# Down projections of two gated feed-forward layers by Strassen's seven block products, on one core

## The chip, the cores and the metric

One Trainium2 chip, one of its cores. The metric is the device time of one execution in microseconds (us). The kernel before takes 1410.69 us as the median of three runs (1410.56 to 1411.05).

## The reference

Two decoder layers on 512 tokens with 1024 features, in float32. The mixers (a state-space scan with stick-breaking attention, then an mLSTM) are not touched by the change. Behind each mixer stands the same feed-forward block, and its down projection is what changes:

```python
def conv_ffn(h, up_w, conv_w, conv_b, down_w):
    u = causal_dwconv(h @ up_w, conv_w, conv_b)
    gate, val = jnp.split(u, 2, axis=-1)
    return (jax.nn.silu(gate) * val) @ down_w
...
        h = h + conv_ffn(rmsnorm(h, norm_w[layer, 1]), ffn_up_w[layer], ffn_conv_w[layer],
                         ffn_conv_b[layer], ffn_down_w[layer])
```

`up_w` is 1024 x 5632, `down_w` is 2816 x 1024, the convolution has width 3.

## The kernel before, in words

Activations lie with features on the 128 partitions and the 512 tokens along the free dimension: `h` is 8 tiles of 128x512, and the gated product of a feed-forward block is 22 tiles (`FF`). A tile of the program is named by what it holds, and the profile and the listings use these names.

**Three products for one.** Float32 operands are split into a rounded part and a rest, both in the type fp32r: `hi` and `lo` for weights, `sh` and `sl` for a gated tile, `xnh` and `xnl` for a normed one. `split` (L505) is a copy on ScalarE (ACT) and a subtraction on VectorE (DVE). `mm3` (L499) multiplies hi x hi, hi x lo and lo x hi into one PSUM bank, so each 128x128 block of weights costs three matmuls of 512 columns on TensorE (PE), each with its own weight load.

**Weights.** They come as units of up to 128x1024 in the order of use. `prefetch` (L482) loads a unit into one of 2 `raw` buffers (`RAW_BUFS`), ACT copies it to `hi`, DVE subtracts to get `lo`; 5 pairs of `hi` and `lo` are kept (`W_BUFS`). `unit` (L493) hands out the next pair.

**The feed-forward block** is `ffn` (L1121). For each of 22 j it forms two up tiles (gate and value): `feat` (L522) runs 24 matmuls over the 8 normed input tiles; DVE multiplies the bank with the norm's row factor `rb` (into `u`); ACT writes the first convolution tap into `c`, DVE adds the other two taps; ACT applies SiLU to the gate; DVE multiplies gate and value; `split` makes `sh`, `sl`. When all 22 are there, each of 8 output tiles takes 66 matmuls in one bank, from three weight units (`DOWN`, L97), and one DVE addition into `h[c]`. In the last block `h[c]` is then stored.

**What follows block 0** is the norm of layer 1 (`norm`, L586): for each `h[k]`, ACT and DVE make `xnh` and `xnl`, ACT squares, DVE sums into `acc`; `rstd` (L567) multiplies `acc` with a column of ones on PE (8 matmuls of 2 columns into `tt`), DVE scales (`var`), GpSimd (POOL) takes the power, DVE spreads the result (`rep`), PE transposes it 4 times. Meanwhile PE runs the first matmuls of layer 1 (`ml_v`, L974: blocks of 24 matmuls of 264 columns into banks `pj`), whose banks are emptied with the factor `rstd`.

**Banks and order.** PSUM has 8 banks: 4 for the name `pj`, 4 shared by `yy`, `zz` and `tt` (L466). The program is first recorded, then `Recorder.order` (L305) gives the instructions of all engines one order from a table of costs (`cost`, L279): at each step the engine that can start first takes its earliest ready call. That order is then fixed: every engine works its own list from front to back. The instructions are issued from one line, L422, so the profile tells them apart by tiles alone.

```python
W_BUFS = 5
RAW_BUFS = 2
SLOTS = 71
```

Of the kernel before, what the change touches and what calls it, by code (L numbers as in the profile page):

```python
# [22 lines left out]
P = 128  # L23
T = 512
# [3 lines left out]
FF = 22  # L28
# [15 lines left out]
def _units(i):  # L44

    hy, ml = i["hy_in_w"][0], i["ml_in_w"][0]
    u = []
    qw, kw, vw = hy[:, 2576:3600], hy[:, 3600:4624], hy[:, 4624:5648]
    xbc, z = _feat(hy[:, 1024:2560]), _feat(hy[:, 0:1024])
    wo = i["hy_out_w"][0]  # L50
    oa, ob = _feat(wo[:1024]), _feat(wo[1024:])
    for kind, n in [x for _, xs in L0_PLAN for x in xs]:
        if kind == "xbc":
            u.append(xbc[n])
        elif kind == "kqv":
            c = slice(P * n, P * n + P)
            dt = hy[:, 2560:2576] if n == 0 else hy[:, 0:0]
            m = np.concatenate([kw[:, c], qw[:, c], vw[:, c], dt], axis=1)
            u += _tok(m) if n else list(m.reshape(KD, P, -1))
        elif kind == "z":  # L60
            u.append(z[n])
        elif kind == "a":
            u.append(oa[n])
    u += ob
    u += _ffn_units(i, 0)
    q, k, v, o = _feat(ml[:, 0:512]), _feat(ml[:, 512:1024]), ml[:, 1024:2048], _feat(ml[:, 2048:3072])
    for kind, n in L1_ORDER:
# [12 lines left out]
    u += _feat(i["ml_out_w"][0])  # L80
    u += _ffn_units(i, 1)
    return u


def _ffn_units(i, l):
    u = []
    up = _feat(i["ffn_up_w"][l])
    for j in range(FF):
        u += [up[j], up[FF + j]]
    dn = i["ffn_down_w"][l]  # L90
    parts = [_feat(dn[a:b]) for a, b in DOWN]
    for c in range(8):
        u += [p[c] for p in parts]
    return u


DOWN = [(0, 1024), (1024, 2048), (2048, 2816)]  # L97

X = lambda kind, *ns: [(kind, n) for n in ns]
# [133 lines left out]
class Pool:  # L235
# [27 lines left out]
class Recorder:  # L263
# [165 lines left out]
W_BUFS = 5  # L429
RAW_BUFS = 2  # L430
# [4 lines left out]
class Net:  # L435
    def __init__(self, tc, pools, xT, w, sizes, pp, off, cc, out):
        self.nc = Recorder()
        self.const, self.wp, self.slots, self.small, self.psp, self.dram = pools
        self.xT, self.out = View(xT, xT.shape), View(out, out.shape)
        self.off = off  # L440
        self.w, self.sizes = View(w, w.shape), sizes
        self.wpos, self.wi = 0, 0
        self.wq = []
        self.n = 0
        nc = self.nc
        c = self.const.tile([P, C_N], F32, name="cc")
# [24 lines left out]
        o = self.off[name] + n  # L471
        return self.pp[:, o : o + w]

    def load_unit(self, tile):
        n = self.sizes[self.wi]
        src = self.w[self.wpos : self.wpos + P * n].rearrange("(p n) -> p n", p=P)
        self.wpos += P * n
        self.wi += 1
        self.nc.sync.dma_start(tile[:, 0:n], src)
        return tile[:, 0:n]  # L480

    def prefetch(self, held=0):  # L482
        nc = self.nc
        while self.wi < len(self.sizes) and len(self.wq) + held < W_BUFS:
            raw = self.load_unit(self.wp.tile([P, 1024], F32, tag="raw", bufs=RAW_BUFS, name=self.name("raw")))
            n = raw.shape[-1]
            hi = self.wp.tile([P, 1024], F32R, tag="hi", bufs=W_BUFS, name=self.name("hi"))[:, 0:n]
            lo = self.wp.tile([P, 1024], F32R, tag="lo", bufs=W_BUFS, name=self.name("lo"))[:, 0:n]
            nc.scalar.copy(hi, raw)
            nc.vector.tensor_tensor(lo, raw, hi.bitcast(F32), op=ALU.subtract)  # L490
            self.wq.append((hi, lo))

    def unit(self, held=0):  # L493
        self.prefetch(held)
# [1 line left out]
        self.prefetch(held + 1)  # L496
        return u

    def mm3(self, ps, a, b, start, stop):  # L499
        mm = self.nc.tensor.matmul  # L500
        mm(ps, a[0], b[0], start=start, stop=False)
        mm(ps, a[0], b[1], start=False, stop=False)
        mm(ps, a[1], b[0], start=False, stop=stop)

    def split(self, src, s="x", n=T):  # L505

# [614 lines left out]
    def ffn(self, l, h, last):  # L1121
        nc = self.nc
        xs, _, _, rb = self.norm(h, f"nw{l}1")
        ss = []
        for j in range(FF):
            cc = []
            for part in range(2):
                n = j + part * FF
                ps = self.ps(("pj", "zz", "yy")[self.n % 3])
                self.feat(ps, xs)  # L1130
                u, c = self.slot("u"), self.slot("c")
                nc.vector.tensor_tensor(u, ps, rb, op=ALU.mult)
                nc.scalar.activation(c, u, AF.Identity, scale=self.param(f"fw{l}2", n), bias=self.param(f"fb{l}", n))
                for d in (1, 2):
                    nc.vector.scalar_tensor_tensor(c[:, d:T], u[:, 0 : T - d], self.param(f"fw{l}{2 - d}", n), c[:, d:T],
                                                   op0=ALU.mult, op1=ALU.add)
                cc.append(c)
            nc.scalar.activation(cc[0], cc[0], AF.Silu)
            nc.vector.tensor_tensor(cc[1], cc[0], cc[1], op=ALU.mult)
            ss.append(self.split(cc[1], "s"))  # L1140
        for c in range(8):
            ps = self.ps(("pj", "zz", "yy", "tt")[c % 4])
            k0 = 0
            for a, b in DOWN:
                k1 = k0 + (b - a) // P
                self.feat(ps, ss[k0:k1], start=k0 == 0, stop=k1 == FF)
                k0 = k1
            nc.vector.tensor_tensor(h[c], ps, h[c], op=ALU.add)
            if last:
                nc.sync.dma_start(self.out[c], h[c])  # L1150
# [188 lines left out]
def prepare(inputs):  # L1339
    i = {k: np.asarray(v) for k, v in inputs.items()}  # L1340
    units = _units(i)
    sizes = [u.size // P for u in units]
    w = np.concatenate([u.reshape(-1) for u in units])
    pp, off = _params(i)
    xT = np.ascontiguousarray(i["x"][0].T).reshape(KD, P, T)
    return {"xT": xT, "w": w, "pp": pp, "cc": _consts()}, sizes, off
# [15 lines left out]
```

## Time and profile before

| what | value |
|---|---|
| median of three runs | 1410.69 us (1410.56 to 1411.05) |
| the profiled execution, its own time | 1410.06 us |
| its span, first to last instruction | 1408.3 us |
| PE busy | 1397.9 us, 99% |
| DVE busy | 989.2 us, 70% |
| ACT busy | 742.3 us, 53% |
| granted TensorE clock | 1.0 throughout |

The span is 1.8 us shorter than the execution's own time, which holds what lies ahead of the first and behind the last instruction. An engine's busy time is the union of its instructions, and an instruction of PE or DVE is still counted while the next one has begun: so a busy share says less than the distance from one start to the next.

### The profile page before, as it was taken

To read this page: it belongs to the slowest core of one execution; us is meant where nothing else is said; L and a number is where in the kernel's file an instruction comes from. 1 tells how busy PE (TensorE), PEld (TensorE's weight loads), DVE (VectorE), ACT (ScalarE), POOL (GpSimd) and SP (SyncE) were. 2 spreads that over 40 slices of the span, in tenths; PEclk is the share of its full clock that TensorE was granted. 3 is DMA by queue.
4 is the path that set the end of the run, shared out by engine and by line. 5 is a ranking of instruction groups with operands and counts; after the bars stand their busy time and mean duration, and the time that the engine had idled before them with its cause. 6 is when DMAs were issued, how large, how long until landed. Compare 5 with 4: busy or idle time off the path is not lost.

```text
span 1408.3 us, 18392 instructions
## 1 busy us (share of the span) xinstructions
PE 1397.9 (99%) x6915; PEld 1170.1 (83%) x6915; DVE 989.2 (70%) x1659; ACT 742.3 (53%) x1229; POOL 58.9 (4%) x140
## 2 busy tenths in 40 slices
PE   9999999999999999999999999999999999999998
PEld 8898999989788888888888898888888888888887
DVE  7999889999987676677623347799767777675221
ACT  7798987886665444444422236685444444443110
POOL 0000001211120000000000000010000000000000
PEclk9999999999999999999999999999999999999999
DMA  6423323234213223323233225232223223223330
GB/s 217 128 76 120 91 61 101 65 91 150 83 31 120 90 90 99 96 90 104 83 98 94 72 76 170 70 109 78 85 90 105 90 90 103 93 86 105 109 102 33
DMA packets 44393, 135.27 MB, mean 96 GB/s; under 512 B 5112, under 2 KB 6136, under 8 KB 44304
## 3 DMA queue, kind: packets, MB, share of 16 engines
q1 hardware_dynamic: 44304, 134.09, 30.5%
q8 instruction: 54, 0.88, 0.3%
q14 instruction: 35, 0.29, 0.1%
HBM read 128.78 MB, written 2.15 MB: 93 GB/s over the span
## 4 chain that ended last, share of the span: by engine, by line
PE 88%; DVE 5%; ACT 3%; issue 3%; DMA 1%; POOL 0%; SPq 0%; DVEq 0%; POOLq 0%; ACTq 0%
PE pj L422 42%; PE yy L422 20%; PE zz L422 17%; PE tt L422 8%; DVE gt L422 1%; DVE wt L422 1%; DVE lo L422 1%; DVE wTl L422 1%; DMA E<-mrow 0%; ACT L422 0%; ACT E L422 0%; ACT Kh L422 0%; POOL wt L422 0%; DMA w<-in_w 0%; ACT Q L422 0%
## 5 line engine op out<-in xcount | busy, mean ns | idle before, releaser
L422 ACT CAST hi<-raw 128x1024 fp32r<-128x1024 f32 (+2 forms) x236 | 234.7, 997 | 269.5 <-PE pj L422 75.9
L422 DVE TENSOR_TENSOR lo<-raw,hi 128x1024 fp32r<-128x1024 f32 (+2 forms) x236 | 272.4, 1156 | 135.3 <-ACT hi L422 135.0
L422 PE MATMUL pj<-xnh,hi 128*128 128x512 f32 x544 | 216.8, 398 | 0.0
L422 PE MATMUL pj<-xnh,lo 128*128 128x512 f32 x544 | 215.9, 397 | 0.0
L422 PE MATMUL pj<-xnl,hi 128*128 128x512 f32 x544 | 215.4, 396 | 0.0
L422 DVE SCALAR_TENSOR_TENSOR c<-u,pp,c 128x511 f32<-128x511 f32 (+2 forms) x212 | 158.0, 748 | 3.5 <-ACT c L422 0.5
L422 PEld LDWEIGHTS pj<-xnh,lo 128*128 128x128 f32 x544 | 102.3, 188 | 22.1
L422 PEld LDWEIGHTS pj<-xnl,hi 128*128 128x128 f32 x544 | 102.3, 188 | 21.4
L422 PEld LDWEIGHTS pj<-xnh,hi 128*128 128x128 f32 x544 | 102.3, 188 | 21.3 <-issue 0.2
L422 PE MATMUL pj<-lo,xnh 128*128 128x384 f32 (+2 forms) x320 | 108.6, 340 | 0.0
L422 PE MATMUL pj<-hi,xnl 128*128 128x384 f32 (+2 forms) x320 | 107.2, 335 | 0.0
L422 PE MATMUL pj<-hi,xnh 128*128 128x384 f32 (+2 forms) x320 | 106.8, 338 | 0.0
L422 PE MATMUL zz<-xnh,lo 128*128 128x512 f32 x224 | 88.4, 394 | 0.0
L422 PE MATMUL yy<-xnh,lo 128*128 128x512 f32 x224 | 88.4, 394 | 0.0
L422 PE MATMUL yy<-xnh,hi 128*128 128x512 f32 x224 | 88.3, 394 | 0.0
L422 PE MATMUL zz<-xnh,hi 128*128 128x512 f32 x224 | 88.3, 394 | 0.0
L422 PE MATMUL yy<-xnl,hi 128*128 128x512 f32 x224 | 88.2, 394 | 0.0
L422 PE MATMUL zz<-xnl,hi 128*128 128x512 f32 x224 | 88.2, 394 | 0.0
L422 ACT CAST sh<-c 128x512 fp32r<-128x512 f32 x44 | 27.3, 620 | 113.5 <-DVE c L422 113.5
L422 ACT ACTIVATE c<-c 128x512 f32<-128x512 f32 x56 | 35.3, 631 | 96.9 <-DVE c L422 96.8
L422 ACT ACTIVATE c<-u,pp 128x512 f32<-128x512 f32 x100 | 81.4, 816 | 1.2 <-DVE u L422 0.9
L422 DVE TENSOR_TENSOR u<-pj,rb 128x512 f32<-128x512 f32 x44 | 30.4, 691 | 48.4 <-PE pj L422 44.2
(363 smaller groups left out, 2977.2 us busy)
## 6 DMA issues: line engine op xcount, KB each, us to landing
raw<-in_w SPq DMA_DIRECT2D x184, 512.0 KB, 3.6
raw<-in_w SPq DMA_DIRECT2D x44, 384.0 KB, 3.1
h<-in_xT SPq DMA_DIRECT2D x16, 256.0 KB, 4.4
E<-acsd SPq DMA_DIRECT2D x16, 256.0 KB, 4.0
raw<-in_w SPq DMA_DIRECT2D x8, 264.0 KB, 2.7
Kl<-Kl SPq DMA_DIRECT2D x16, 128.0 KB, 2.2
E<-mrow SPq DMA_DIRECT2D x8, 256.0 KB, 5.4
out_h<-h SPq DMA_DIRECT2D x8, 256.0 KB, 2.0
```

The lines of the kernel that those rows point to most:

```text
L422: getattr(getattr(nc, c.engine), c.method)(*(r(a) for a in c.args), **{k: r(v) for k, v in c.kw.items()})
```

## The change

In both feed-forward blocks the down projection of the first 20 of 22 feature tiles is done in blocks of 2 feature tiles x 2 output tiles x 2 token halves. Instead of 8 block products there are 7 (`11`, `21`, `n1`, `n2`, `t3`, `t4`, `22`), each on 256 tokens; their operands are sums and differences of weight blocks (`P1` to `P4`, made by DVE in `weight_tiles`) and of token halves (`F` and `G`, made by DVE in `token_sums` and split anew). `down_blocks` runs them for one pair of output tiles (c = 0 to 3) and one chunk of features (8, 8 or 4 tiles), summing over the chunk's pairs in PSUM; seven DVE additions or subtractions of 256 columns take the banks into `h`, and a bank that was read is multiplied into again. The chunks stand between the up projections (`FFN_PLAN`); the last two feature tiles go the old way in `down_rest`, 6 matmuls of 512 columns for each output tile. The bytes of weights are the same; they are laid out in another order.

```diff
 def _ffn_units(i, l):
     u = []
     up = _feat(i["ffn_up_w"][l])
-    for j in range(FF):
-        u += [up[j], up[FF + j]]
     dn = i["ffn_down_w"][l]
-    parts = [_feat(dn[a:b]) for a, b in DOWN]
-    for c in range(8):
-        u += [p[c] for p in parts]
+    for kind, n in FFN_PLAN:
+        if kind == "up":
+            u += [up[n], up[FF + n]]
+        elif kind == "down":
+            a, b = CHUNKS[n]
+
+            t = dn[a * P : b * P].reshape((b - a) // 2, 2, P, 4, 2, P).transpose(3, 2, 4, 1, 0, 5)
+            u += [x.reshape(P, 4, (b - a) // 2, P) for x in t]
+        else:
+            t = dn[REST * P :].reshape(FF - REST, P, 8, P).transpose(1, 2, 0, 3)
+            u += [t[:, 4 * k : 4 * k + 4].reshape(P, -1, P) for k in range(2)]
     return u
...
+CHUNKS = [(0, 8), (8, 16), (16, 20)]
+REST = 20
+FFN_PLAN = [("up", j) for j in range(9)] + [("down", 0)] + [("up", j) for j in range(9, 17)] + [("down", 1)]
+FFN_PLAN += [("up", j) for j in range(17, FF)] + [("down", 2), ("rest", 0)]
...
+    def split_weights(self, parts):
+
+        hi, lo = (self.wp.tile([P, 1024], F32R, tag=t, bufs=W_BUFS, name=self.name(t)) for t in ("hi", "lo"))
+        a = 0
+        for p in parts:
+            s = slice(a, a + p.shape[-1])
+            self.nc.scalar.copy(hi[:, s], p)
+            self.nc.vector.tensor_tensor(lo[:, s], p, hi[:, s].bitcast(F32), op=ALU.subtract)
+            a = s.stop
+        return hi[:, 0:a], lo[:, 0:a]
+
+    def weight_tiles(self):
+
+        v = self.nc.vector
+        while self.wi < len(self.sizes):
+            n, blocks = self.sizes[self.wi]
+            if not blocks:
+                yield self.split_weights([self.load_unit(self.raw_tile())])
+                continue
+            src, kb, raws = self.next_unit(), n // 4, []
+            for a in range(0, n, 1024):
+                raws.append(self.raw_tile())
+                self.nc.sync.dma_start(raws[-1], src[:, a : a + 1024])
+            per = 1024 // kb
+            w = lambda i, m=1: raws[i // per][:, i % per * kb : (i % per + m) * kb]
+            tile = lambda s: self.slot(s, n=kb)
+            p1, p2 = tile("P1"), tile("P2")
+            if per == 2:
+                yield self.split_weights([w(0, 2)])
+            v.tensor_tensor(p1, w(2), w(3), op=ALU.add)
+            v.tensor_tensor(p2, p1, w(0), op=ALU.add)
+            yield self.split_weights([p2, p1] if per == 2 else [w(0, 2), p2, p1])
+            p3, p4 = tile("P3"), tile("P4")
+            v.tensor_tensor(p3, w(0), w(2), op=ALU.add)
+            v.tensor_tensor(p4, p2, w(1), op=ALU.add)
+            if per == 2:
+                yield self.split_weights([p3, p4])
+                yield self.split_weights([w(3)])
+            else:
+                yield self.split_weights([p3, p4, w(3)])
...
     def ffn(self, l, h, last):
         nc = self.nc
         xs, _, _, rb = self.norm(h, f"nw{l}1")
-        ss = []
-        for j in range(FF):
+        pairs, ss, first = {}, [], None
+        for kind, j in FFN_PLAN:
+            if kind == "down":
+                a, b = CHUNKS[j]
+                for c in range(4):
+                    self.down_blocks([pairs[k] for k in range(a // 2, b // 2)], h, c)
+                continue
+            if kind == "rest":
+                self.down_rest(ss, h, last)
+                continue
             cc = []
...
             nc.scalar.activation(cc[0], cc[0], AF.Silu)
             nc.vector.tensor_tensor(cc[1], cc[0], cc[1], op=ALU.mult)
-            ss.append(self.split(cc[1], "s"))
+            if j >= REST:
+                ss.append(self.split(cc[1], "s"))
+            elif j % 2:
+                pairs[j // 2] = self.token_sums(first, cc[1])
+            else:
+                first = cc[1]
+
+    def token_sums(self, c1, c2):
+
+        v = self.nc.vector
+        a, b = slice(0, T // 2), slice(T // 2, T)
+        t = self.slot("B11", F32R)
+        self.nc.scalar.copy(t[:, a], c1[:, a])
+        v.tensor_tensor(t[:, b], c1[:, a], t[:, a].bitcast(F32), op=ALU.subtract)
+        s2 = self.split(c2, "s")
+        f, g = self.slot("F"), self.slot("G")
+        v.tensor_tensor(f[:, a], c1[:, a], c1[:, b], op=ALU.subtract)
+        v.scalar_tensor_tensor(f[:, b], c2[:, b], -1.0, f[:, a], op0=ALU.mult, op1=ALU.subtract)
+        fs = self.split(f, "F")
+        v.tensor_tensor(g[:, a], c2[:, b], c1[:, b], op=ALU.subtract)
+        v.scalar_tensor_tensor(g[:, b], f[:, b], -1.0, c2[:, a], op0=ALU.mult, op1=ALU.subtract)
+        gs = self.split(g, "G")
+        half = lambda t, s: (t[0][:, s], t[1][:, s])
+        return {"11": (t[:, a], t[:, b]), "21": half(s2, a), "22": half(s2, b),
+                "n1": half(fs, a), "n2": half(fs, b), "t3": half(gs, a), "t4": half(gs, b)}
+
+    def down_blocks(self, xs, h, c):
+
+
+
+
+        v = self.nc.vector
+        kb, n = len(xs) * P, T // 2
+        a, b = slice(0, n), slice(n, T)
+        X, Z, Y = (self.ps(t)[:, 0:n] for t in (("pj", "yy", "zz"), ("yy", "pj", "pj"))[c % 2])
+        h1, h2 = h[2 * c], h[2 * c + 1]
+        at = {"i": 0, "u": None}
+
+        def product(ps, form, more=False):
+            i, per = at["i"], 1024 // kb
+            if i % per == 0:
+                at["u"] = self.unit()
+            hi, lo = at["u"]
+            at["i"] = i + 1
+            for k, x in enumerate(xs):
+                s = slice(i % per * kb + k * P, i % per * kb + k * P + P)
+                self.mm3(ps, (hi[:, s], lo[:, s]), x[form], not more and k == 0, k == len(xs) - 1, skip_group_check=more)
+
+        add = lambda o, ps, op=ALU.add: v.tensor_tensor(o, o, ps, op=op)
+        product(X, "11")
+        product(Z, "21")
+        add(h1[:, a], X)
+        product(X, "n2", True)
+        add(h1[:, a], Z)
+        product(Y, "n1")
+        add(h1[:, b], X)
+        product(X, "t3", True)
+        add(h2[:, b], Y, ALU.subtract)
+        product(Y, "22", True)
+        add(h2[:, b], X, ALU.subtract)
+        product(X, "t4", True)
+        add(h1[:, b], Y)
+        add(h2[:, a], X, ALU.subtract)
+
+    def down_rest(self, ss, h, last):
+        nc, n = self.nc, len(ss) * P
         for c in range(8):
+            if c % 4 == 0:
+                hi, lo = self.unit()
+            s = slice(c % 4 * n, c % 4 * n + n)
             ps = self.ps(("pj", "zz", "yy", "tt")[c % 4])
-            k0 = 0
-            for a, b in DOWN:
-                k1 = k0 + (b - a) // P
-                self.feat(ps, ss[k0:k1], start=k0 == 0, stop=k1 == FF)
-                k0 = k1
+            self.feat(ps, ss, (hi[:, s], lo[:, s]))
             nc.vector.tensor_tensor(h[c], ps, h[c], op=ALU.add)
             if last:
                 nc.sync.dma_start(self.out[c], h[c])
```

Names in the lists below: a tile's name, then its number; out before the arrow, inputs behind it.

**VectorE at the last chunk.** Before, DVE's list in the down stage of block 0 holds little (`lo`: rest of a weight unit, `h`: the addition of a finished output tile, `xnl`: the next norm's operand):

```order
L422 TENSOR_TENSOR lo_1479_7254<-raw_1477_7196,hi_1478_7246 128x1024
L422 TENSOR_TENSOR h_849_4024<-pj_1470_7176,h_849_4024 128x512
L422 TENSOR_TENSOR lo_1483_7280<-raw_1481_7231,hi_1482_7270 128x1024
L422 SCALAR_TENSOR_TENSOR xnl_1552_7291<-h_849_4024,pp_78,xnh_1551_7283 128x512
L422 TENSOR_TENSOR lo_1486_7315<-raw_1484_7262,hi_1485_7308 128x768
L422 TENSOR_TENSOR lo_1489_7346<-raw_1487_7294,hi_1488_7338 128x1024
```

Now, from the last up tile on (`u`, bank `yy_1653`), with the weights (`raw`, `P2`, `lo`) and the additions into `h` (tiles 849 to 856) of the chunk of 4 tiles:

```order
L433 TENSOR_TENSOR u_1658_8374<-yy_1653_8296,rb_1161_5481 128x512
L433 TENSOR_TENSOR lo_1669_8384<-raw_1665_8274,hi_1668_8360 128x512
L433 TENSOR_TENSOR h_849_4024<-h_849_4024,pj_1662_8364 128x256
L433 TENSOR_TENSOR h_849_4024<-h_849_4024,yy_1663_8379 128x256
L433 SCALAR_TENSOR_TENSOR c_1659_8393<-u_1658_8374,pp_78,c_1659_8393 128x511
L433 TENSOR_TENSOR lo_1669_8384<-P2_1667_8339,hi_1668_8360 128x256
L433 SCALAR_TENSOR_TENSOR c_1659_8393<-u_1658_8374,pp_78,c_1659_8393 128x510
L433 TENSOR_TENSOR h_849_4024<-h_849_4024,pj_1662_8364 128x256
L433 TENSOR_TENSOR c_1659_8393<-c_1652_8310,c_1659_8393 128x512
L433 TENSOR_TENSOR lo_1669_8384<-P1_1666_8316,hi_1668_8360 128x256
L433 TENSOR_TENSOR lo_1673_8458<-P3_1670_8321,hi_1672_8416 128x256
L433 TENSOR_TENSOR h_850_4059<-h_850_4059,zz_1664_8390 128x256
```

Between `u_1658` and the addition of the product `n2` in bank `yy_1674` (second row `h_851<-h_851,yy_1674`) stand 26 instructions, itself among them; before, an output tile of 66 matmuls had about six instructions of DVE beside it.

**TensorE in the same chunk.** Bank `yy_1674` (first of the pair c = 1) takes product `n2` (the last three rows of it are shown; operand `F`) and right behind it `t3` (operand `G`):

```order
L433 MATMUL yy_1674_8402<-Fh_1624_8208,hi_1649_8246 128x256
L433 MATMUL yy_1674_8402<-Fl_1625_8222,hi_1649_8246 128x256
L433 MATMUL yy_1674_8402<-Fh_1624_8208,lo_1650_8261 128x256
L433 MATMUL yy_1674_8402<-Gh_1593_8063,hi_1656_8293 128x256
L433 MATMUL yy_1674_8402<-Gl_1594_8073,hi_1656_8293 128x256
L433 MATMUL yy_1674_8402<-Gh_1593_8063,lo_1657_8306 128x256
```

The `G` rows write into the bank that DVE reads after the `F` rows: they wait for that addition, with nothing put in between. 84 matmuls of 256 columns stand between the last up matmul (`yy_1653`) and the first `G` row of this bank.

**TensorE at the norm after block 0.** Before, 20 matmuls of 264 columns stand between the last product with the column of ones and the four transposes of `rep` (the last three are shown), and more of them follow:

```order
L422 MATMUL pj_1590_8022<-lo_1549_7934,xnh_1563_7840 128x264
L422 MATMUL pj_1590_8022<-hi_1548_7928,xnl_1564_7856 128x264
L422 MATMUL pj_1590_8022<-hi_1548_7928,xnh_1565_7970 128x264
L422 MATMUL tt_1580_8063<-cc_205,rep_1579_8048 128x128 x4
L422 MATMUL pj_1590_8022<-lo_1549_7934,xnh_1565_7970 128x264
L422 MATMUL pj_1590_8022<-hi_1548_7928,xnl_1566_7985 128x264
L422 MATMUL pj_1592_8072<-hi_1538_7803,xnh_1551_7283 128x264
```

Now the four blocks `pj` are through by then, and the transposes follow the ones at once; the next block (`pj_1774`) needs a bank that DVE empties with the factor `rstd`:

```order
L433 MATMUL tt_1742_8918<-ones_r_259,acch_1743_8904 128x2
L433 MATMUL tt_1742_8918<-ones_r_259,accl_1744_8916 128x2
L433 MATMUL tt_1748_8944<-cc_205,rep_1747_8935 128x128 x4
L433 MATMUL pj_1774_8956<-hi_1752_8824,xnh_1719_8673 128x264
L433 MATMUL pj_1774_8956<-lo_1753_8837,xnh_1719_8673 128x264
L433 MATMUL pj_1774_8956<-hi_1752_8824,xnl_1720_8689 128x264
```

The work that stood between ones and transposes now stands ahead of both.

## Rows read from the trace of the kernel before

**Rows 1.** The page, part 1: busy time, share of the span, instructions.

```profile
span 1408.3 us, 18392 instructions
PE 1397.9 (99%) x6915; PEld 1170.1 (83%) x6915; DVE 989.2 (70%) x1659; ACT 742.3 (53%) x1229; POOL 58.9 (4%) x140
PEclk9999999999999999999999999999999999999999
```

**Rows 2.** Stretches: length, busy by engine with instructions, clock, DMA; up and down stages.

```profile
core 0: us, PE busy (x) PEld busy (x) DVE busy (x) ACT busy (x) POOL busy (x), PEclk, DMA share, GB/s
455.00:690.00 235.00, 235.00 (x1024) 190.89 (x1023) 165.40 (x213) 102.34 (x128) 1.01 (x1) 1.00 0.31 95
1282.00:1404.70 122.70, 122.70 (x528) 98.77 (x527) 30.98 (x32) 20.64 (x22) 0.00 (x0) 1.00 0.27 86
```

**Rows 3.** Timeline of PE at 95 us: start, length, instruction.

```profile
95.28 0.28 PE L422 MATMUL yy<-xel,bth 128*128 128x256 f32 x1
...
95.99 0.28 PE L422 MATMUL yy<-xeh,btl 128*128 128x256 f32 x1
96.10 0.34 PE L422 MATMUL pj<-lo,xnh 128*128 128x384 f32 x1
```

**Rows 4.** A stretch of PE alone, with 264-column matmuls only: length, busy, matmuls.

```profile
831.20:841.20 10.00, 10.00 (x84) 1.00 0.48 148
```

**Rows 5.** Timeline at the norm after block 0: matmuls of 2 columns with their loads.

```profile
826.12 0.25 PE L422 MATMUL tt<-ones_r,accl 128*128 128x2 f32 x1
826.23 0.25 PE L422 MATMUL tt<-ones_r,acch 128*128 128x2 f32 x1
826.32 0.19 PEld L422 LDWEIGHTS tt<-ones_r,accl 128*128 128x128 f32 x1
826.35 0.25 PE L422 MATMUL tt<-ones_r,accl 128*128 128x2 f32 x1
```

**Rows 6.** Timeline of DVE in an up stage.

```profile
502.96 0.69 DVE L422 TENSOR_TENSOR u<-yy,rb 128x512 f32<-128x512 f32 x1 [1.31 <-PE yy L422]
503.57 0.68 DVE L422 TENSOR_TENSOR sl<-c,sh 128x512 fp32r<-128x512 f32 x1
504.17 1.22 DVE L422 TENSOR_TENSOR lo<-raw,hi 128x1024 fp32r<-128x1024 f32 x1
505.31 1.53 DVE L422 SCALAR_TENSOR_TENSOR c<-u,pp,c 128x511 f32<-128x511 f32 x2
```

**Rows 7.** Groups of DVE by shape: count, busy us, mean ns.

```profile
L422 DVE TENSOR_TENSOR st<-yy,st 128x256 f32<-128x256 f32 x8 | 3.4, 422 | 0.1
```

**Rows 8.** Timeline: a handover from PE to DVE (819 us), one from DVE to PE (935 us).

```profile
819.31 0.39 PE L422 MATMUL tt<-sh,lo 128*128 128x512 f32 x1
819.73 0.69 DVE L422 TENSOR_TENSOR h<-tt,h 128x512 f32<-128x512 f32 x1 [2.98 <-PE tt L422]
...
935.72 0.34 DVE L422 SCALAR_TENSOR_TENSOR num<-yy,wint,num 128x130 f32<-128x130 f32 x1
...
936.21 0.30 PE L422 MATMUL yy<-Q,kh 128*128 128x128 f32 x1 [0.91 <-DVE num L422]
```

**Rows 9.** Timeline of DVE and POOL at the norm after block 0, behind the ones.

```profile
826.63 0.16 DVE L422 TENSOR_SCALAR var<-tt 128x4 f32<-128x4 f32 x1 [2.68 <-PE tt L422]
826.88 1.01 POOL L422 TENSOR_TENSOR rstd<-var,mhalf 128x4 f32<-128x4 f32 x1 [20.29 <-DVE var L422]
...
827.92 0.43 DVE L422 COPY rep<-rstd 128x512 f32<-128x512 f32 x1 [1.12 <-POOL rstd L422]
828.42 0.23 DVE L422 SCALAR_TENSOR_TENSOR gates<-pj,rstd,pp 128x8 f32<-128x8 f32 x1
828.57 0.87 DVE L422 SCALAR_TENSOR_TENSOR v<-pj,rstd,v 128x256 fp32r<-128x256 f32 x2
```

**Rows 10.** DMA issues: KB each, median us to landing.

```profile
raw<-in_w SPq DMA_DIRECT2D x184, 512.0 KB, 3.6
```

More of the change, by code (lines that the diff above doesn't have):

```diff
@@ L87, in _ffn_units @@
     up = _feat(i["ffn_up_w"][l])
-    for j in range(FF):
-        u += [up[j], up[FF + j]]
     dn = i["ffn_down_w"][l]
-    parts = [_feat(dn[a:b]) for a, b in DOWN]
-    for c in range(8):
-        u += [p[c] for p in parts]
-    return u
-DOWN = [(0, 1024), (1024, 2048), (2048, 2816)]
+    for kind, n in FFN_PLAN:
[8 more added lines that the diff above has]
+            u += [t[:, 4 * k : 4 * k + 4].reshape(P, -1, P) for k in range(2)]
+    return u
+CHUNKS = [(0, 8), (8, 16), (16, 20)]
+REST = 20
+FFN_PLAN = [("up", j) for j in range(9)] + [("down", 0)] + [("up", j) for j in range(9, 17)] + [("down", 1)]
+FFN_PLAN += [("up", j) for j in range(17, FF)] + [("down", 2), ("rest", 0)]
 X = lambda kind, *ns: [(kind, n) for n in ns]
@@ L442, in __init__ @@
         self.wpos, self.wi = 0, 0
-        self.wq = []
+        self.wq, self.wtiles = [], self.weight_tiles()
         self.n = 0
@@ L472, in param, with next_unit @@
         return self.pp[:, o : o + w]
-    def load_unit(self, tile):
-        n = self.sizes[self.wi]
+    def next_unit(self):
+        n = self.sizes[self.wi][0]
         src = self.w[self.wpos : self.wpos + P * n].rearrange("(p n) -> p n", p=P)
@@ L478, in load_unit @@
         self.wi += 1
-        self.nc.sync.dma_start(tile[:, 0:n], src)
-        return tile[:, 0:n]
-    def prefetch(self, held=0):
[L483 to L491, printed above, removed]
+        return src
@@ new lines, in load_unit, with raw_tile @@
+    def load_unit(self, tile):
+        src = self.next_unit()
+        tile = tile[:, 0 : src.shape[-1]]
+        self.nc.sync.dma_start(tile, src)
+        return tile
+    def raw_tile(self):
+        return self.wp.tile([P, 1024], F32, tag="raw", bufs=RAW_BUFS, name=self.name("raw"))
+    def split_weights(self, parts):
[7 more added lines that the diff above has]
+        return hi[:, 0:a], lo[:, 0:a]
@@ L493, in unit @@
+    def prefetch(self, held=0):
+        while len(self.wq) + held < W_BUFS:
+            u = next(self.wtiles, None)
+            if u is None:
+                return
+            self.wq.append(u)
     def unit(self, held=0):
@@ L497, in unit, with mm3 @@
         return u
-    def mm3(self, ps, a, b, start, stop):
+    def mm3(self, ps, a, b, start, stop, **kw):
         mm = self.nc.tensor.matmul
-        mm(ps, a[0], b[0], start=start, stop=False)
-        mm(ps, a[0], b[1], start=False, stop=False)
-        mm(ps, a[1], b[0], start=False, stop=stop)
+        mm(ps, a[0], b[0], start=start, stop=False, **kw)
+        mm(ps, a[0], b[1], start=False, stop=False, **kw)
+        mm(ps, a[1], b[0], start=False, stop=stop, **kw)
     def split(self, src, s="x", n=T):
@@ L1341, in prepare @@
     units = _units(i)
-    sizes = [u.size // P for u in units]
+    sizes = [(u.size // P, u.ndim == 4) for u in units]
     w = np.concatenate([u.reshape(-1) for u in units])
```

## The prediction

> **What bounds the kernel now.** I read the page first: TensorE (PE) is busy for 99% of the span, VectorE (DVE) for 70%, and the granted clock is 1.0 throughout, which is the upper of its two levels, 2.4 GHz [rows 1]. A busy share hides how dense the work is, so next I read stretches: the down stage of block 1 runs 528 matmuls of 512 columns in 122.7 us, one every 0.2324 us without a hole [rows 2]. So in both down stages time is matmuls times their distance, and a matmul less is time less, as long as what feeds PE keeps up. Third, I read how far apart shorter matmuls stand, since the change halves their columns [rows 3 to 5]. Fourth, I read DVE by the distance from one start to the next, since an instruction's length overlaps the next one's: a length of 0.68 us for 512 columns stands for a distance of 0.60, a length of 1.22 for 1.14, two taps of 510 columns take 1.44 together [rows 6]. So about 0.085 us of each length is overlap, and 256 columns, length 0.422 [rows 7], cost 0.335.
>
> **PE: the gain.** Per layer, 20 of 22 feature tiles need 20 x 8 x 3 = 480 matmuls of 512 columns before: 480 x 0.2324 = 111.5 us. Now 10 pairs of feature tiles x 4 pairs of output tiles x 7 products x 3 = 840 matmuls of 256 columns. Seven matmuls of 256 columns run from 95.28 to 96.10 us, 0.117 each [rows 3]; 84 of 264 columns fill 10.0 us, 0.119 to 0.121 each [rows 4]. I take 0.118: 840 x 0.118 = 99.1 us. Gain 12.4 us per layer, **24.8 us** for both. The last two feature tiles cost the same as before (48 matmuls), and so does the up projection (24 matmuls a tile).
>
> What speaks against a halved matmul is its weight load, which does not get shorter. Rows show its floor: matmuls of only 2 columns, each with its own load of 128 columns, start 0.11 us apart [rows 5]. That lies under 0.118, by little. The Trainium skill ("TensorE: Matmul & The Clock Gate", Back-to-back issue gap) says that in a real stream both weight load and matmul set the spacing, and gives 131 ns at 512 columns against 81 at 128; a straight line between them would be an estimate of 98 at 256, so 21 matmuls would cost more than 12 did, and by that rule the change would lose. This trace disagrees: its 512 columns stand 232 ns apart, not 131, and 256 stand at half of that. I go by the rows.
>
> **DVE: the load.** For one pair of output tiles and a chunk of 8 tiles, DVE splits weights (one instruction of 1024 columns, five of 512), forms four sums of 512 and adds seven banks of 256: 1.14 + 3.0 + 2.4 + 2.35 = 8.9 us, beside 84 x 0.118 = 9.9 us of PE. For the chunk of 4 tiles: one split of 512, five of 256, four sums of 256, seven additions: 0.6 + 1.68 + 1.34 + 2.35 = 6.0 us beside 42 x 0.118 = 5.0 us. An up tile pair costs 2 x 1.14 + 2 x 0.6 + 2 x 1.44 + 0.6 = 7.0 us, as before, and token sums now 3.6 us per two j where two splits took 1.2; so 8.8 us beside 48 x 0.2324 = 11.2 us of PE. In sum DVE does some 290 of 356 us of PE per layer. The up stages and the chunks of 8 cover it, the chunk of 4 does not. ScalarE's added copies lie under PE: it is busy for 102 of 235 us in an up stage and 21 of 123 in a down stage [rows 2]. Weights are loaded in the same bytes, 512 KB landing in 3.6 us [rows 10], against two such loads per 9.9 us; SP's queue carries two issues fewer per layer. I cost both at nothing; with only two raw buffers, the next pair's load waits until this pair's sums are formed, and if that cover were gone each chunk would wait for part of a 3.6 us landing.
>
> *Chunks of 8.* Each bank is read by DVE and multiplied into again one product later, so a product of 12 matmuls (1.42 us) covers the addition. Handover from PE to DVE takes the rest of the last matmul and almost nothing more (819.31 + 0.39, start 819.73), and from DVE to PE about 0.15 us (935.72 + 0.34, start 936.21) [rows 8]: 0.2 + 0.42 + 0.15 = 0.77 us with DVE idle. One split of 1024 in front adds 1.14 and breaks the cover by half a microsecond. Following the order from the last up tile on, DVE is mostly ahead; I take 0.5 us for each of four chunks, **2 us**. Ends: 0, and 2 us each, if DVE's lengths counted instead of distances.
>
> *Chunk of 4.* Cover is 0.71 us, less than the 0.77 above. The tightest place is bank `yy_1674`: PE reaches product `t3` after 84 matmuls, 9.9 us behind the last up tile. DVE has until then 25 instructions (5 of 512, 18 of 256, the two taps: 3.0 + 6.0 + 1.44 = 10.5 us) and then the addition: 0.2 + 10.5 + 0.42 + 0.15 = 11.3 us, and about 0.6 more in which DVE itself waits for product `22` in bank `zz_1664`. PE waits 2 us. After this the rest's matmuls of 512 columns slot in and DVE, 22 us of work up to the chunk's end against 19.8 of PE, is level again. **4 us** for both layers; ends 1 and 6 us a layer.
>
> *The norm after block 0.* Before, finished tiles came 15 us apart and the norm's work lay under PE. Now all eight finish within 8 x 6 x 0.2324 = 11 us, and each needs an addition, an `xnl` and a sum on DVE. PE starts layer 1 about 0.4 us late for its last operands. Then the chain from the ones to a free bank stands bare: before, 826.35 (last ones) to 828.57 + 0.48 (bank emptied) = 2.7 us [rows 5, 9] lay under 20 and more matmuls of 264 columns; now PE has the transposes and nothing else there. Some 2.6 us. Together **3 us**, once; ends 1 and 5. Block 1 has no norm behind it, and its last addition and store stay as they are.
>
> **Sum.** -24.8 + 2 + 4 + 3 = -15.8 us, against the profiled execution's own 1410.06 us: 1394.3. That execution lies 0.6 us under the median of the runs, so I predict 1394.9 us.
>
> **Rivals.**
> 1. *DVE is the bound.* If its lengths counted (0.69, 0.42, 1.22 in place of 0.60, 0.335, 1.14), a chunk of 8 would need 10.4 us against PE's 9.9, and the chunk of 4 7.4 against 5.0; my walk along the order then gives 2 us of waiting for each chunk of 8 and 6 for each of 4: 20 + 3 back of 24.8, so 1408.9 us, no change. Against it: starts 0.60 apart [rows 6]. The Trainium skill ("VectorE: DVE Perf Modes", The DRAIN you can't avoid) says that the next instruction does not start until the pipe is empty, and allows an earlier start for one that is not held. These rows show the earlier start. 9%.
> 2. *Handover per bank, slower than before.* There are 7 x 12 x 2 = 168 products whose banks DVE must read. A mean wait above (24.8 - 3) / 168 = 0.13 us per product eats the gain. If queued splits sit in front of most additions, say 0.2 us each, 34 us: 1423 us. For it: covers of 0.71 us in the chunk of 4 and no slack in front of `yy_1674`; against it: in the chunks of 8 the order puts one to two other products between. 7%.
> 3. *The weight load sets the pace.* If loads were bared for these matmuls, each would take the load's own 0.19 us [rows 5]: 1680 x (0.19 - 0.118) = 121 us more, 1516 us. It turns to a loss from 0.131 us a matmul on. Against it: rows 3 and 4, with the same load. 2%.
>
> **How the numbers follow.** My forecast of a gain between no waits at all (1386) and twice the waits that I sum (1404) gets 82%. About 0.2%, or 2.8 us, is what a measurement of this kernel can tell from no change. Rival 1 is within it or near it, rivals 2 and 3 are slower: faster 0.83, same 0.08, slower 0.09. Range 1387 to 1404: below it only a distance under 0.118 helps; above it lie the rivals.
>
> **What would show it.** Right: PE's matmuls of 256 columns 0.118 us apart in the chunks of 8; up stages unchanged; PE idle behind DVE `h` by 1 to 3 us in each chunk of 4, and by 2 to 3 us behind DVE (`rep`, `v`) at the norm after block 0; DVE near 290 us of distances per layer. Wrong: idle time of PE behind `lo` or `h` in the chunks of 8 (rival 1 or 2), behind DMA of `raw` (two buffers too few), or a distance well above 0.118 with no wait named (rival 3).

## The result: 1395.3 us, 1.1% faster

The changed kernel takes 1395.28 us (median of four runs, 1394.39 to 1395.61) against 1410.62 us (1409.91 to 1411.05) for the kernel before: a ratio of 0.9891, 95% interval 0.9878 to 0.9905. The forecast was 1394.9 us, range 1387 to 1404. The profiled execution took 1394.39 us, its span is 1392.6 us, 15.7 us shorter than that of before.

The page, part 1, of the changed kernel (answers to [rows 1]):

```profile
span 1392.6 us, 20550 instructions
PE 1376.1 (99%) x7635; PEld 1190.6 (85%) x7635; DVE 1177.4 (85%) x2143; ACT 793.1 (57%) x1369; POOL 58.5 (4%) x140
```

PE is still busy for 99%, with 720 matmuls more and 21.8 us less of busy time. DVE has gained 188 us of busy time and stands at 85%. The page alone would not say whether that is harmless, so the stages are read next, in stretches: the first chunk of 8 feature tiles, the chunk of 4 of each layer, and the norm after block 0; below them the same norm in the kernel before.

```profile
core 0: us, PE busy (x) PEld busy (x) DVE busy (x) ACT busy (x) POOL busy (x), PEclk, DMA share, GB/s
553.15:594.01 40.86, 40.86 (x343) 40.65 (x341) 36.39 (x66) 16.78 (x25) 0.00 (x0) 1.00 0.34 115
777.07:801.15 24.08, 22.71 (x178) 21.73 (x177) 22.06 (x52) 9.21 (x18) 0.00 (x0) 1.00 0.30 94
1355.50:1379.10 23.60, 22.21 (x176) 21.31 (x175) 21.66 (x51) 8.12 (x16) 0.00 (x0) 1.00 0.20 68
810.16:839.60 29.44, 26.58 (x205) 26.00 (x204) 18.33 (x36) 11.97 (x21) 1.01 (x1) 0.94 0.25 80
```

```profile
819.50:844.30 24.80, 24.80 (x205) 24.76 (x204) 12.40 (x26) 11.11 (x18) 1.01 (x1) 1.00 0.27 86
```

- The chunk of 8: PE has no hole in 40.86 us. Its 336 block matmuls at 0.118 us and five up matmuls among them at 0.2324 make 40.8.
- The chunks of 4: PE idles 1.4 us in each, and with the slower restarts each takes about 2.15 us more than its matmuls at their distances (168 of 256 columns, 9 and 7 of 512).
- The norm: the same 205 instructions of PE take 29.4 us where they took 24.8, PE idles 2.9 of them, and the mean granted clock is 0.94.

By kind of matmul and layer, distances from start to start summed over the feed-forward block from the transposes of `rep` on, from the two traces:

| stretch | before | after | difference |
|---|---|---|---|
| layer 0, up matmuls (1014) | 234.7 | 234.8 | 0.0 |
| layer 0, down (528; 840 + 48) | 122.4 | 101.5 + 11.1 | -9.8 |
| first to last of 192 matmuls of 264 columns at the norm | 24.7 | 29.4 | +4.7 |
| layer 1, up matmuls (1016) | 236.9 | 235.5 | -1.4 |
| layer 1, down (528; 840 + 48) | 122.5 | 101.5 + 10.9 | -10.2 |

These make -16.7 us. The remaining +1.0 lies in three places: the mixer between norm and next feed-forward block is 0.3 longer, the tail behind the last matmul 0.3, what lies ahead of layer 0's block 0.4. The -1.4 of layer 1 comes from up matmuls that stood 233.1 ns apart before and stand 231.8 apart now, near the 231.5 of layer 0 in both kernels; no run tells why.

PE's waits, longest sums first (engine, output tile, releaser, us in total, times, longest). Of these rows the kernel before has the one behind `wt` alone:

```profile
PE yy L433 <- DVE h L433: 2.7, 2, 1.4
PE tt L433 <- DVE wt L433: 2.1, 4, 1.3
PE tt L433 <- DVE rep L433: 1.8, 1, 1.8
...
PE tt L433 <- DVE accl L433: 0.6, 1, 0.6
PE pj L433 <- DVE v L433: 0.5, 1, 0.5
```

So all new waits have the places that the prediction named: `h` once in each chunk of 4, and the chain at the norm.

**The wait in the chunk of 4.** Timeline of PE and of DVE around it (start, length, instruction, idle time before and releaser):

```profile
788.76 0.39 PE L433 MATMUL yy<-Gh,hi 128*128 128x256 f32 x1 [1.35 <-DVE h L433]
788.98 0.28 PE L433 MATMUL yy<-Gl,hi 128*128 128x256 f32 x1
```

```profile
784.95 0.42 DVE L433 TENSOR_TENSOR h<-h,zz 128x256 f32<-128x256 f32 x1 [0.33 <-PE zz L433]
...
787.02 0.69 DVE L433 TENSOR_TENSOR lo<-raw,hi 128x512 fp32r<-128x512 f32 x1
787.63 0.41 DVE L433 TENSOR_TENSOR h<-h,pj 128x256 f32<-128x256 f32 x1
787.96 0.42 DVE L433 TENSOR_TENSOR P<-P,raw 128x256 f32<-128x256 f32 x1
788.29 0.41 DVE L433 TENSOR_TENSOR h<-h,yy 128x256 f32<-128x256 f32 x1
```

It is the first `G` row of bank `yy_1674`, as forecast: DVE has no idle time in front of `h<-h,yy`, it is late with all that stands before it. The starts show DVE's distances once more, 0.61 for 512 columns and 0.33 for 256, as in [rows 6]. From DVE's end to PE's start lie 0.06 us.

**The norm.** Timeline of PE behind the last output tile of block 0:

```profile
821.84 0.27 PE L433 MATMUL tt<-ones_r,acch 128*128 128x2 f32 x1
822.67 0.27 PE L433 MATMUL tt<-ones_r,accl 128*128 128x2 f32 x1 [0.55 <-DVE accl L433]
...
823.36 0.25 PE L433 MATMUL tt<-ones_r,accl 128*128 128x2 f32 x1
...
825.41 0.91 PE L433 MATMUL tt<-cc,rep 128*128 128x128 f32 x4 [1.80 <-DVE rep L433]
826.82 0.56 PE L433 MATMUL pj<-hi,xnh 128*128 128x264 f32 x1 [0.50 <-DVE v L433]
827.17 0.42 PE L433 MATMUL pj<-lo,xnh 128*128 128x264 f32 x1
827.39 0.42 PE L433 MATMUL pj<-hi,xnl 128*128 128x264 f32 x1
...
829.25 0.28 PE L433 MATMUL pj<-hi,xnl 128*128 128x264 f32 x1
829.37 0.29 PE L433 MATMUL pj<-hi,xnh 128*128 128x264 f32 x1
```

DVE's timeline there:

```profile
824.93 0.43 DVE L433 COPY rep<-rstd 128x512 f32<-128x512 f32 x1 [1.12 <-POOL rstd L433]
825.44 0.23 DVE L433 SCALAR_TENSOR_TENSOR gates<-pj,rstd,pp 128x8 f32<-128x8 f32 x1
825.58 0.70 DVE L433 TENSOR_TENSOR lo<-raw,hi 128x528 fp32r<-128x528 f32 x1
826.19 0.87 DVE L433 SCALAR_TENSOR_TENSOR v<-pj,rstd,v 128x256 fp32r<-128x256 f32 x2
```

and stretches of the same kernel there (columns as above), the waiting, the transposes and what follows:

```profile
824.00:825.60 1.60, 0.19 (x2) 0.19 (x3) 0.59 (x3) 1.30 (x3) 0.90 (x1) 1.00 0.53 200
825.70:826.80 1.10, 0.62 (x4) 0.23 (x3) 1.10 (x3) 1.10 (x4) 0.00 (x0) 0.50 0.02 7
826.90:829.00 2.10, 2.10 (x10) 2.10 (x11) 2.10 (x7) 1.02 (x2) 0.00 (x0) 0.50 0.72 246
829.20:831.20 2.00, 2.00 (x19) 2.00 (x19) 0.35 (x2) 0.00 (x0) 0.00 (x0) 1.00 0.35 84
```

First the sum of squares is late (`accl`), then the chain over GpSimd and `rep` stands bare, as forecast, and `v` after it. In DVE's list a split of a weight unit (`lo`, 528 columns) now stands between `gates` and `v`, 0.61 us from start to start, where `v` followed `gates` at once before [rows 9]. What was not forecast comes behind: PE has waited 0.55 and 1.80 us and was busy for 1.16 of the 3.5 us up to 825.4; then the granted clock falls to 0.5, the lower level of 1.2 GHz, and stays there until about 829.1. Matmuls of 264 columns start 0.22 us apart in that time (the first two 0.35), and 0.12 once the clock is back.

### The profile page after: what moved, and what is told of

Same layout as the page of the kernel before. It is cut to its first block, busy times and chain, and to the rows that moved or that the text cites. A ratio compares the mean times of both kernels' runs of the same rounds, so it can differ in the third digit from the quotient of the medians.

```text
span 1392.6 us, 20550 instructions
## 1 busy us (share of the span) xinstructions
PE 1376.1 (99%) x7635; PEld 1190.6 (85%) x7635; DVE 1177.4 (85%) x2143; ACT 793.1 (57%) x1369; POOL 58.5 (4%) x140
## 3 DMA queue, kind: packets, MB, share of 16 engines
HBM read 128.78 MB, written 2.15 MB: 94 GB/s over the span
## 4 chain that ended last, share of the span: by engine, by line
PE 83%; issue 7%; DVE 6%; ACT 3%; POOL 1%; DMA 0%; SPq 0%; POOLq 0%; DVEq 0%; ACTq 0%
PE pj L433 46%; PE yy L433 23%; PE zz L433 10%; PE tt L433 4%; DVE gt L433 1%; DVE wt L433 1%; DVE lo L433 1%; DVE wTl L433 0%; ACT L433 0%; DMA h<-in_xT 0%; ACT Kh L433 0%; POOL wt L433 0%; ACT Q L433 0%; DVE ss L433 0%; ACT hi L433 0%
## 5 line engine op out<-in xcount | busy, mean ns | idle before, releaser
L433 ACT CAST hi<-raw 128x1024 fp32r<-128x1024 f32 (+4 forms) x240 | 226.7, 947 | 262.1 <-PE pj L433 77.9
L433 DVE TENSOR_TENSOR lo<-raw,hi 128x1024 fp32r<-128x1024 f32 (+4 forms) x240 | 261.9, 1094 | 18.7 <-ACT hi L433 17.6
L433 PE MATMUL pj<-xnh,lo 128*128 128x512 f32 x592 | 234.8, 397 | 0.0
L433 PE MATMUL pj<-xnl,hi 128*128 128x512 f32 x592 | 234.7, 396 | 0.0
L433 PEld LDWEIGHTS pj<-xnh,hi 128*128 128x128 f32 x592 | 111.4, 188 | 23.5 <-issue 0.2
L433 PE MATMUL yy<-xnl,hi 128*128 128x512 f32 x272 | 107.2, 394 | 0.0
L433 ACT CAST hi<-P 128x512 fp32r<-128x512 f32 (+1 forms) x96 | 50.7, 546 | 85.6 <-DVE P L433 44.6
L433 PEld LDWEIGHTS pj<-hi,xnh 128*128 128x128 f32 x320 | 60.6, 190 | 2.6 <-PE tt L433 0.9
L433 PEld LDWEIGHTS pj<-lo,xnh 128*128 128x128 f32 x320 | 60.8, 190 | 1.6 <-DVE lo L433 0.2
L433 PEld LDWEIGHTS pj<-hi,xnl 128*128 128x128 f32 x320 | 60.6, 190 | 1.5
L433 PEld LDWEIGHTS yy<-xnl,hi 128*128 128x128 f32 x272 | 51.1, 188 | 11.8
L433 PEld LDWEIGHTS yy<-xnh,hi 128*128 128x128 f32 x272 | 51.1, 188 | 11.8
```

What stands on the lines that cost most here:

```text
L433: getattr(getattr(nc, c.engine), c.method)(*(r(a) for a in c.args), **{k: r(v) for k, v in c.kw.items()})
```

## The experiments

The open questions were: is the price per matmul as read, is DVE really no bound in the chunks of 8 (rival 1) or the banks (rival 2), and are the two places named the whole of what was given back? Each diff is against the changed kernel, but for the first; `...` marks left-out lines.

**Half matmuls alone.** The kernel before, with each down matmul of 512 columns cut into two of 256, in two banks. Nothing is saved, so only the price of shorter matmuls is left.

```diff
...
-                self.feat(ps, ss[k0:k1], start=k0 == 0, stop=k1 == FF)
+                hi, lo = self.unit()
+                for k in range(k0, k1):
+                    w = slice((k - k0) * P, (k - k0 + 1) * P)
+                    for ps, t in zip(banks, halves):
+                        self.mm3(ps, (hi[:, w], lo[:, w]), (ss[k][0][:, t], ss[k][1][:, t]), k == 0, k == FF - 1)
...
```

> The kernel before, with each 512-column matmul of the two down projections cut into two of 256 columns (two banks, two additions of 256 instead of one of 512); no block products, no sums. My theory: 1056 matmuls per layer at the 0.118 us that the chunks of 8 show, instead of 528 at 0.2324: 2 x (1056 x 0.1182 - 122.7) = +4.2 us, so 1414.8 us. Rival (the weight load sets the pace of narrow matmuls): at 0.131 us a matmul, where the change would have gained nothing, +31 us, 1442 us; at the load's own 0.19 us, 1566 us.

It took 1415.56 us (1415.04 to 1415.73), ratio 1.0032 (1.0020 to 1.0044). The down stage of block 0 as one stretch:

```profile
697.00:822.00 125.00, 125.00 (x1056) 124.87 (x1055) 42.75 (x56) 31.41 (x40) 1.27 (x24) 1.00 0.27 84
```

125.00 / 1056 = 0.1184 us a matmul, without a hole, 1056 in a row: the weight load sets no pace at 256 columns, and rival 3 falls. Two halves cost 0.2368 against 0.2324, which over 1056 matmuls of both layers makes 4.6 of the 4.9 us measured.

**Another bank at the norm.** The second half of `ml_v`'s blocks goes to `yy` rather than `pj`, so PE need not wait there for a `pj` bank to be emptied with `rstd`.

```diff
-                ps = self.ps()
+                ps = self.ps("yy" if part == (1,) else "pj")
```

> The change, and the second half of layer 1's first value projection takes banks of the other four (yy) instead of pj, so that TensorE has matmuls to run while the norm's factor is made. My theory: the change's loss at the norm after block 0 (matmuls of 264 columns last 29.35 us from first to last there, 24.67 before) is TensorE waiting with no bank free, and the lowered clock behind that wait: it falls to 25 to 26 us, the time by 4 us to 1391.3. Rival (the norm's own work on VectorE is late, whatever TensorE has to do): the stretch stays over 28 us and the time at 1395.

It took 1389.56 us (1389.22 to 1393.08), ratio 0.9854 (0.9839 to 0.9868), 5.7 us less than the change alone, where 4 were expected. The two profiled executions differ by 4.8 us (1394.39 and 1389.56), all of it at the norm; the change's was the fastest of its four. The stretch from the last output tile on, and PE's timeline in it:

```profile
810.16:835.00 24.84, 24.84 (x206) 24.81 (x205) 18.09 (x36) 11.97 (x21) 1.01 (x1) 1.00 0.28 96
```

```profile
822.23 0.17 PE L433 MATMUL tt<-ones_r,acch 128*128 128x2 f32 x1
822.26 0.37 PE L433 MATMUL yy<-hi,xnh 128*128 128x264 f32 x1
```

The matmuls of `yy` run on between the ones, PE has no hole, the clock stays at 1.0, and 192 matmuls take 24.6 us as before. So the norm's loss was a matter of banks: work for PE was at hand, but had nowhere to go. The lower clock goes with the waits in all traces: the five that have them at this norm (the change, and below the sums on GpSimd, all chunks of 4 and both ballasts) show it for 3.4 us, one of them for 6.8, and the five without them show none there. But one of the four executions of this version took 1393.08 us, at a mean clock of 0.997 against 0.999 or more in the others; it has no trace, so what happened in it stays open.

**The sums of the chunk of 4 on GpSimd.**

```diff
             tile = lambda s: self.slot(s, n=kb)
...
+            v = self.nc.vector if per == 2 else self.nc.gpsimd
```

> The change, with the sums P1 to P4 of the chunk of 4 tiles made by GpSimd instead of VectorE. My theory: TensorE's 2 us of waiting in each chunk of 4 come from VectorE's queue: 16 sums of 0.335 us (5.4 us) leave it, the 1.5 us wait in front of product t3 falls under 0.5 us, and 3 to 4 us are won: 1391.5 us. Rival (GpSimd is slow at this, and the splits then wait for its sums): TensorE waits for lo instead of h and the time is 1397 us or more.

It took 1393.48 us (1393.08 to 1394.26), ratio 0.9877 (0.9862 to 0.9891): 1.8 us under the change, half of what was expected. The two waits of 1.4 us at `yy` are gone from PE's list, others have come, still behind `h` (first row; the second is one of GpSimd's two groups of sums, with count, busy us and mean ns):

```profile
PE pj L433 <- DVE h L433: 1.2, 2, 0.6
```

```profile
L433 POOL TENSOR_TENSOR P<-raw 128x256 f32<-128x256 f32 x16 | 16.1, 1024 | 614.6 <-DMA raw<-in_w 614.6
```

The two chunks of 4 took 23.5 (with one more of 512 columns) and 22.8 us where they took 24.1 and 23.6: each still takes 1.3 us more than its matmuls at their distances. A sum of 256 columns takes GpSimd 1.02 us in the mean, where DVE needs 0.33, and DVE itself is slower beside them. Two splits of 256 columns in a row, in the change and then here, with GpSimd's sums around them:

```profile
781.92 0.76 DVE L433 TENSOR_TENSOR lo<-P,hi 128x256 fp32r<-128x256 f32 x2
```

```profile
781.18 1.99 POOL L433 TENSOR_TENSOR P<-raw 128x256 f32<-128x256 f32 x2 [4.62 <-DMA raw<-in_w]
782.50 1.84 DVE L433 TENSOR_TENSOR lo<-P,hi 128x256 fp32r<-128x256 f32 x2
783.14 0.91 POOL L433 TENSOR_TENSOR P<-P,raw 128x256 f32<-128x256 f32 x1
```

DVE loses 1.1 us at these two, right ahead of an addition from bank `zz` that PE waits for, and has no idle time from there to the longer of the new waits at 789.25. DVE's additions from a bank keep their 0.41 us beside GpSimd's sums. So part of what left DVE's list came back as slower splits; how much of the missing half that makes, no run separates.

**Both of these.** Together they hit different places, so their gains should add.

> The change with both edits, the yy banks for the second half of the value projection and the sums of the chunk of 4 on GpSimd. If the two waits are separate, their gains add: 1389.6 - 1.8 = 1387.8 us. If one hides the other (what is won in the chunk of block 0 is lost again at the norm behind it), 1389.5 us.

It took 1388.23 us (1386.65 to 1389.35), ratio 0.9838 (0.9824 to 0.9851): the fastest version of this study, 22 us under the kernel before and 7 under the change. By the medians the two gains nearly add (5.7 + 1.8 = 7.5 expected from the parts, 7.1 found). In its list of PE's waits the norm's are gone, but those in the chunks of 4 sum to 2.7 us, as in the change:

```profile
PE zz L433 <- DVE h L433: 1.5, 2, 0.8
...
PE pj L433 <- DVE h L433: 1.2, 2, 0.6
```

Its chunks of 4 take 24.04 (with one more of 512 columns) and 23.37 us, where the version with the other bank alone has 24.10 and 23.61. So of the 1.7 us that the sums on GpSimd won in the chunks by themselves, the trace has 0.5 here; another 0.5 of the 1.3 us between the two medians lies ahead of the first feed-forward block, which neither edit touches. That the gains add is not shown.

**No chunk of 4.** The last 6 feature tiles go the old way, in place of 2.

```diff
-CHUNKS = [(0, 8), (8, 16), (16, 20)]
-REST = 20
+CHUNKS = [(0, 8), (8, 16)]
+REST = 16
...
```

The rest's weights come as one unit of 768 columns for each output tile.

> The change without the chunk of 4: tiles 16 to 21 go the old way (18 matmuls of 512 columns for each output tile, weights in 8 units of 768). My theory: per layer 96 x 0.2324 - 168 x 0.1182 = +2.45 us of matmuls, -2.15 us of waits in the chunk of 4; and finished tiles come 4.2 us apart instead of 1.4, so the 4.7 us lost at the norm come back: 1395.3 + 4.9 - 4.3 - 4.7 = 1391.2 us. Rival (the waits are not the chunk's own): they move to the rest stage, and only the matmuls count: 1400 us.

It took 1391.30 us (1389.28 to 1393.02), ratio 0.9861 (0.9844 to 0.9877). Per layer it gives up 4/20 of 12.4 = 2.5 us and saves the 2.15 us of waiting, which is nearly a draw; the gain of 4 us over the change is the norm's, where the trace has 4.7. The last output tiles come 18 x 0.2324 = 4.2 us apart rather than 1.4, and its stretch at the norm takes 24.6 us. Its list of PE's waits has no row behind `h`, `rep`, `accl` or `v`. So the chunk of 4 earns next to nothing here, and the norm can be mended by the order as well as by banks.

**All chunks of 4.** Five of them in each layer, each between the up projections, at least one up tile pair behind its last input.

```diff
-CHUNKS = [(0, 8), (8, 16), (16, 20)]
+CHUNKS = [(4 * k, 4 * k + 4) for k in range(5)]
...
```

> The change with five chunks of 4 tiles per layer in place of 8, 8 and 4; the matmuls are the same in number and width. My theory: a chunk of 4 asks 6.0 us of VectorE for 5.0 us of TensorE and has one product, 0.71 us, to cover a bank's addition, so each of the ten chunks waits about 2.15 us as the two do now: +17 us, 1412.5 us, all the gain gone. Rival (the wait belongs to the last chunk, where the last up tile's convolution and the rest's weights share VectorE's queue): 1395 to 1398 us.

It took 1412.36 us (1411.16 to 1413.38), ratio 1.0011 (1.0002 to 1.0020): the whole gain is lost. PE's waits behind `h`:

```profile
PE yy L435 <- DVE h L435: 10.1, 10, 1.4
PE pj L435 <- DVE h L435: 2.9, 8, 0.4
```

Eight chunks of 4 stand where four of 8 stood, and the time is 17.1 us longer than the change's, 2.1 for each: the price that the trace of the change shows for its own two, 2.15. The matmuls are the same in number (7635); in the trace each of the ten chunks takes 1.9 to 2.2 us more than its matmuls at their distances, so this is waiting. It is rival 2's mechanism, at chunks that the change has only two of.

**Ballast.** How much slack has DVE in the chunks of 8? Per pair of output tiles three, then seven additions of 256 columns are put on DVE, into a tile that nobody reads.

```diff
+            if per == 2 and i in (0, 2, 4):
+                v.tensor_tensor(self.slot("ballast", n=n), self.cc[:, 0:n], self.cc[:, n : 2 * n], op=ALU.add)
```

(with seven: `i in range(7)`)

> The change, and in the chunks of 8 VectorE runs 3 more additions of 256 columns (constants, into a tile nobody reads) for each pair of output tiles: 12 x 0.335 = 4.0 us in each chunk, where the trace shows VectorE busy for 36.4 of 41 us. My theory: that nearly uses up its slack of 4.6 us; 0 to 0.7 us of waiting in each of four chunks, 1395 to 1398 us. Rival (VectorE is the bound already, only hidden in other names): each added microsecond costs one, +16 us, 1411 us.

> The same with 7 such additions for each pair: 28 x 0.335 = 9.4 us in each chunk. My theory: 9.4 - 4.6 = 4.8 us over in each of four chunks, +19 us, 1414 us. If VectorE can take up more of it in the up stages (weights made earlier, additions put off), as little as +8 us, 1403 us; if VectorE was the bound already, +38 us, 1433 us.

With three (1.0 us per pair) the time is 1397.26 us (1396.89 to 1397.57), ratio 0.9902 (0.9889 to 0.9916), 2.0 over the change; each chunk of 8 takes 0.3 to 0.7 us more than its matmuls at their distances (0.1 in the change), and PE's list has no new row of a wait. With seven (2.3 us per pair, 9.4 per chunk) it is 1405.18 us (1403.86 to 1406.27), ratio 0.9958 (0.9944 to 0.9971), 9.9 over it, and the list has:

```profile
PE zz L433 <- ACT hi L433: 4.6, 4, 1.2
PE zz L433 <- DVE h L433: 3.1, 4, 0.8
```

once per chunk of 8 each. So a chunk of 8 has room for about 1 us more per pair of output tiles, and not for 2.3. The 9.9 us are the waits: the chunk's stretch is 46.6 us long with 336 block matmuls and 19 up matmuls (5 before, the order pulls more of them in), whose distances make 44.1, and 2.5 us by four chunks are 10. Of the 9.4 us of ballast in a chunk, 4.5 (40.86 - 36.39) had room in DVE's idle time. The expectation's main figure, +19 us, was twice too high; it did not reckon with the 14 up matmuls more, 14 x 0.2324 = 3.3 us of PE in each chunk under which DVE goes on.

## Why the prediction was right

**The gain on PE: right.** Distances of 0.118 us gave 24.8 us. In the trace, 840 block matmuls take 101.5 us a layer, 99.3 without the 2.15 of waiting that the chunk of 4 holds: 0.1183 each. The half matmuls confirm it by themselves. Of the two spacings weighed in the prediction, that of the rows held. The figures that the Trainium skill gives ("TensorE: Matmul & The Clock Gate", Back-to-back issue gap), 131 ns at 512 columns and 81 at 128, do not show in these runs: 512 columns stand 232 ns apart and 256 stand at 118, half of it.

**DVE by distances, not lengths: right.** Rival 1 would have had PE wait 2 us in each chunk of 8, and it waited none. At 788 us, where PE waited for DVE and DVE had no pause, its starts are 0.33 apart for lengths of 0.42. Of the two things that the Trainium skill says ("VectorE: DVE Perf Modes", The DRAIN you can't avoid), a next instruction that waits for the empty pipe and one that may start earlier, these rows again show the second.

**Chunks of 8: too high.** "I take 0.5 us for each of four chunks" stood for one split of 1024 in front of an addition. It measured 0.1 at most. In the trace of the first chunk DVE waits for PE ahead of six of the 27 additions, 2.9 us in all, and PE never for DVE, and the ballast shows why: DVE has about 1 us of slack per pair of output tiles, more than the half microsecond by which the cover was thought broken.

**Chunk of 4: right.** 2 us a layer at `yy_1674` were forecast, 2.15 found, of it 1.6 from start to start at that very bank (1.35 idle), the rest at two shorter waits beside it, each with a slower first matmul (0.22 us in place of 0.12). The 0.6 us of DVE's waiting for product `22` in bank `zz_1664` is in the trace with 0.33 (784.95 us). That the sum comes so near owes something to luck, since the two shorter waits had not been named.

**The norm: mechanism right, size off.** "Together 3 us" measured 4.7. Counted from start to start, the matmuls with the column of ones and the waits behind them take 3.57 us where they took 0.73, the transposes and the wait for `v` 1.41 rather than 0.35, and the 192 matmuls themselves 24.38 rather than 23.59. So waiting makes 3.9 of the 4.7 (PE's list has 2.9 of it, since it counts from the end of a matmul's length), and the slower matmuls behind it, at the lower clock, make 0.8. The term took the chain at its length before, 2.7 us from the last ones to an emptied bank; from the last ones to the next block's first matmul it now takes 3.46 (823.36 to 826.82), 0.61 of it the split that DVE's list has put between `gates` and `v`. And it had no lower clock in it. At the transposes the lower clock cost nothing, though they took 0.91 us: in the version with seven additions of ballast the clock falls later, at 833.5 us, the transposes take 0.66, and PE waits longer for `v` instead:

```profile
831.93 0.66 PE L433 MATMUL tt<-cc,rep 128*128 128x128 f32 x4 [1.80 <-DVE rep L433]
833.34 0.41 PE L433 MATMUL pj<-hi,xnh 128*128 128x264 f32 x1 [0.76 <-DVE v L433]
```

From start to start these are again 1.41 us.

**The sum.** The two errors, -2 at the chunks of 8 and +1.7 at the norm, cancel, and so nearly do -1.4 in layer 1's up stage and +1.0 elsewhere, which the forecast had at nothing. That the median came within 0.4 us of the forecast is luck; the terms were good to 2 us each. Rival 2 did not happen in the change, and its mechanism takes the whole gain in the neighbour with chunks of 4 alone.

## To carry to other kernels

When a stage that binds TensorE is made shorter, list what its length used to cover: here a norm's chain and DVE's splits. If matmuls are ready but have no free bank, another bank gives the cover back, here 5.7 us for one line. Price a queue by distances from start to start and by the work that stands ahead of one instruction in its engine's list, not by busy shares: DVE at 89% of a chunk of 8 cost nothing, and at 92% of a chunk of 4 it cost 9%. A bare chain can cost more than its length before: here a split had moved into it (0.6 us), and 0.8 us at the lower clock came behind it. Work that is given to another engine can slow the engine it left: here DVE's splits beside GpSimd's sums.

## What the hardware showed that was not expected

- After waits of 0.55 and 1.80 us, with nine matmuls and 1.16 us of busy time from 821.9 to 825.4, the granted clock was 0.50 from about 825.7 to 829.1 us, with 264 columns 0.22 us apart against 0.12. In the chunk of 4, behind one wait of 1.4 us in a dense stream, the stretch has 1.00.
- The first matmul behind a wait holds the next back: 0.22 us to the second against 0.118 (788.76 and 788.98).
- GpSimd took 1.02 us in the mean for a sum of 256 columns in float32, three times DVE's distance. While it ran them, two of DVE's splits of 256 columns took 1.84 us together in place of 0.76; DVE's additions that read a bank kept their 0.41 us each.
